# One more weight unit loaded during the output product, norm rows prepared on GpSimd among the experts, and eighteen units in single transfers

## The chip, the cores and the metric

The kernel runs on one core of a Trainium2 chip. A core has a matrix engine (TensorE, PE in the profile; its weight loads are listed as PEld), a vector engine (VectorE, DVE), a scalar engine (ScalarE, ACT), a general engine (GpSimd, POOL) and a sync engine (SyncE, SP) that here only issues transfers. Sixteen DMA engines move data between the large memory (HBM) and the on-chip memory (SBUF). Each engine runs its own list of instructions in order, and semaphores hold an instruction back until what it needs is there. Matrix products are accumulated in a small memory of banks (PSUM), from which DVE or ACT copy ("evict") them.

The metric is the device time of one execution in microseconds (us); lower is better.

## The reference

One encoder layer on 512 tokens of width 1024, in float32. Three token mixers run side by side (neighbourhood attention, grouped-query attention with rotary positions, attention to 256 memory tokens). Their outputs are gated, summed and multiplied by `w_out`; a residual and a layer norm follow. Then comes the mixture of experts, another residual and another layer norm:

```
merged = sum_g sigmoid(gate_g(x)) * (branch_g @ w_branch[g])
x = layer_norm(DN_ALPHA * x + merged @ w_out, ln1_g, ln1_b)

aff = softmax(x @ w_router)                  # 512 x 16
gate, idx = top_k(aff.T, 64)                 # every expert picks its 64 tokens
xs = x[idx]                                  # 16 x 64 x 1024
h  = xs @ w_gate_up                          # 16 experts, 1024 x 2048 each
y  = (silu(h[:, :1024]) * h[:, 1024:]) @ w_down   # 1024 x 1024 each
x  = layer_norm(DN_ALPHA * x + scatter_add(gate * y), ln2_g, ln2_b)
```

The weights of the sixteen experts are 192 MB in float32, read once each. The four vectors `ln1_g`, `ln1_b`, `ln2_g`, `ln2_b` (the "norm rows") are needed at the ends of both residuals; the host hands them over as 15 rows of 1024, named `lnp`.

## The kernel before

**Stages.** The mixers fill the first part of the execution, up to about 450 us. The output product (`woc`, L1108 to L1112) and, in between its pieces, the router (logits, the top 64 of each expert, one-hot matrices) follow until about 517 us. The expert stage then runs from expert 0 to expert 15, and a final layer norm ends at 962.1 us. All instructions are written out by hand in the order in which each engine runs them; no planner moves them.

**Weight units.** The expert weights are cut into 192 units of 1 MB, each 128 partitions x 2048 numbers: per expert eight units "gu" (a slice of gate and up) and four "dn" (a slice of down). `_blocks()` (L45) lists them in the order of use, where the down product of expert e-1 stands in the middle of the gate/up product of expert e: gu0 0-7, gu1 0-3, dn0 0-3, gu1 4-7, gu2 0-3, dn1 0-3, gu2 4-7, gu3 0-3, dn2 0-3, gu3 4-7, gu4 0-3 and so on. Counted from 0, gu2 2 is unit 22.

**The ring.** The units go into slots which are buffers that the mixers used and no longer need. `RING` (L32) names them: twelve places with room for one or two units, 22 units in all. The first round is loaded during the mixers and the output product, as each place comes free. Three places later leave (`ROUNDS`: "raw" after one round, "VS" and "G1" after two), so 18 slots remain. `Ring.load` (the transfer is L829) issues the next load on SP; `Ring.done` (L850) is called where a unit has been used, and issues the next load as soon as its slot is free. Most loads bring two units in one transfer of 2 MB (a pair), which needs both slots of a place; early units (below 36) and the last ten come in single transfers of 1 MB. Loads wait in SP's list in ring order, each for the PE instructions that last read its slot, and for the landing of the transfer that stands eight before it.

**The pause.** Around the output product SP issues a load into "raw" at 475.70 us, and the next one, into "Q9", at 501.80 us, when the output product has released that buffer.

**The experts.** For expert e, `gate_up` (PE lines L1314: tiles g and u) multiplies the 64 gathered tokens with the gu units. `act_h` (L1319) makes the hidden values: ACT a tanh (L1324, tile tg), DVE two products (L1325 into tg, L1326 into h). `h_transpose` turns h and `down` (PE L1350, tile y) multiplies with the dn units. Before every fourth expert, `gather` (PE L1274 and L1276, tile ga) collects the tokens of the next four experts by one-hot products in eight chunks; they go through three PSUM buffers ("mm"), and their evictions into xs are shared between DVE (L1281) and ACT (L1279). gather(1), for experts 4 to 7, stands right after `act_h(3)` in the program. The tiles tg and h come from the tag "t", which has two buffers that are taken in turn.

**The norm rows.** `load_norms` loads the 15x1024 rows during the mixers into a buffer there; one ACT copy (`norm_hi`, L877) and two DVE operations (`norm_mask` L881, `norm_lo` L884) split them into a high and a low part in the tile gb. Their first use is `ln_row` (PE L1398) in expert four, from 617.3 us.

**Router scratch.** The tile rt (tag "bf") holds the router's small tables. Later "bf" holds GTe, the transposed one-hot matrices of an expert pair made by `slots_T`.

Of the kernel before, what the change touches and what calls it, by code (L numbers as in the profile page):

```python
# [9 lines left out]
F32 = mybir.dt.float32  # L10
# [8 lines left out]
P = 128  # L19
# [25 lines left out]
def _blocks():  # L45
    order = []
    for e in range(NEXP - 1):
        order += [("gu", e, k) for k in range(lead(e))]
        if e:
            order += [("dn", e - 1, k) for k in range(4)]  # L50
        order += [("gu", e, k) for k in range(lead(e), KD)]
    order += [("gu", NEXP - 1, k) for k in range(KD)]
    order += [("dn", e, k) for e in (NEXP - 2, NEXP - 1) for k in range(4)]
    blocks, i, r = [], 0, 0
    while i < len(order):
        for tag, n in RING:
            left = ROUNDS.get(tag, len(order)) - r
            if left > 0 and i < len(order):
                keys = order[i:i + n]
                i += n  # L60
                if r and (i < FULL or i > len(order) - N_SINGLE):
                    blocks += [(tag, h, [key]) for h, key in enumerate(keys)]
                else:
                    blocks.append((tag, 0, keys))
        r += 1
    return blocks

# [2 lines left out]
def layer_kernel(ctx: ExitStack, tc: tile.TileContext, xt, xn, first0, wu, bgate, rpb, gains, wrt,  # L70
# [194 lines left out]
    gb = cp.tile([15, D], F32R, name="gb")  # L265
# [186 lines left out]
    def g_gqa():  # L452
        kk = R("Q6", [P, 4, S], "kk", F32R)
        qs = R("Q4", [P, 8, S], "qs", F32R)
        ST["b01"] = b01 = R("Q5", [P, 4, 1024], "ropevg")
        b1t = b01[:, 2:4]
        vg = b1t[:, 0, :512].rearrange("p (m f) -> p m f", m=NT)
        ST.update(khh=kk[:, 0:2], klo=kk[:, 2:4], vg=vg, qs=(qs[:, 0:4], qs[:, 4:8]),
                  rope=(vs_t[:, 0], b1t[:, 1]), zr=b01[:, 0:2])
        rope = []  # L460
        for q in range(3):
            us = ws.take(2)
            zs = ST["A5" if q % 2 else "A6"][:, 1, :512 if q == 0 else 1024].rearrange("p (m c) -> p m c", m=NT)
# [12 lines left out]
        a, b = rope[1:]  # L476
        bg.extend([lambda: None, a[4], b[0], a[5], b[1], b[2], b[3], norm_hi, b[4], b[5]])

    def g_na_v():
        v = ST["b01"][:, 0:2].rearrange("p a (b f) -> p (a b) f", f=S)  # L480
# [333 lines left out]
    class Ring:  # L814
# [7 lines left out]
        def load(self):  # L822
            tag, h, keys = self.blocks[self.n]
            n = len(keys)
            src = wx[self.row:self.row + P * n].rearrange("(p j) (h c) -> p (j h) c", j=n, h=2)
            if tag not in self.home:
                self.home[tag] = R(tag, [P, 2 * dict(RING)[tag], D], f"w{self.n}")
            full = self.home[tag][:, 2 * h:2 * (h + n)]
            nc.sync.dma_start(full, src)  # L829
# [35 lines left out]
        after[N_UNITS - 14 + 2 * i] = [lambda: ring.more(4)]  # L865
    vs_t = R("VS", [P, 2, 1024], "ropesq")

    norm_raw = []

    def load_norms():  # L870
        norm_raw.append(vs_t[:15, 1])
        nc.sync.dma_start(norm_raw[0], lnp)

    after[14] = [load_norms]

    def norm_hi():
        nc.scalar.copy(gb, norm_raw[0])  # L877

    def norm_mask():
        norm_raw.append(vs_t[:15, 0])  # L880
        nc.vector.tensor_scalar(norm_raw[1], gb.bitcast(F32), gb_c, None, op0=ALU.mult)  # L881

    def norm_lo():
        nc.vector.scalar_tensor_tensor(gb, norm_raw[0], gb_s, norm_raw[1], op0=ALU.mult, op1=ALU.add)  # L884


    run(g_mem())
    dump("mkT", ST["mkT"])
# [9 lines left out]
    bg.extend([norm_mask, norm_lo])  # L898
    run(g_branch(2, True), 1.0, 3)
    run(g_na_v(), 1.0)  # L900
    at.drain()
# [15 lines left out]

    run(g_branch(1, False, between), 0.5)

    rt = R("bf", [P, 12, 64], "rt")  # L920
    aff = rt[:, 0].rearrange("p (m e) -> p m e", m=NT)
    cnt = rt[:, 2:4].rearrange("p a (m e) -> p m a e", m=NT)
    st_all = rt[:, 5:7].rearrange("p a b -> p (a b)")[:, :96].rearrange("p (m q s) -> p m q s", m=NT, q=4)
    ones_f = rt[:, 7:9].rearrange("p a b -> p (a b)")
    nc.gpsimd.memset(ones_f, 1.0)
    lgA = rt[:, 9].rearrange("p (m e) -> p m e", m=NT)
    rb = rt[:, 10][:, :NEXP]
    wsum = rt[:, 10][:, NEXP:3 * NEXP].rearrange("p (a e) -> p a e", a=2)
# [3 lines left out]
    wg_t = rt[:, 2:4].rearrange("p a (k e) -> p (a k) e", e=NEXP)  # L932
    wb_t = rt[:, 0:2].rearrange("p a (k e) -> p (a k) e", e=NEXP)
    wps = []

    def router_scale():
        for i, w in enumerate((wg_t, wb_t)):
# [14 lines left out]
    at.drain()  # L952
    dump("ynh", ST["y0"][0].bitcast(F32))
    dump("macc", ST["macc"])


    mh = R("G0", [P, KD, S], "mh", F32R)
# [24 lines left out]
    tri_t = [rt[:, 4].bitcast(F16), rt[:, 11].bitcast(F16), tri_d]  # L982
# [13 lines left out]
    a01 = R("t", [48, P], "a01", bufs=2)  # L996
    a23 = R("t", [48, 64 + P], "a23", bufs=2)
    nc.gpsimd.memset(a01, 0.0)
    nc.gpsimd.memset(a23, 0.0)
    top = cp.tile([48, 64], F32, name="top")  # L1000

    eps2 = small([P, 2], "eps", bufs=1)
# [5 lines left out]
    mvs, rs_v, rs_h, rs_y, rs_a, nmx, sme, rce = (  # L1008
        small([P, NT, 2] if n == "mv" else [P, NT], "r_" + n, bufs=1) for n in ("mv", "v", "h", "y", "a", "nm", "sm", "rc"))

    def r_transpose(m, k0, n=4):
        t = R("tmp", [P, n, P], f"x1T{m}{k0}", bufs=2)
        tp = PB("T", f"x1t{m}{k0}", (P, n, P))
        for j in range(n):
            k = k0 + j
# [110 lines left out]
    us = ws.take(2)  # L1126
    ws.prefetch(2)
    us += ws.take(2)
    ring.upto(8)

    def w_rest(m, c, n, q, hooks={}):
        acc = PB("S", f"woc{m}{c}")
# [72 lines left out]
    x1_norm(3)  # L1205
    x1_parts(3)
    keep_warm(28)
    ring.upto(len(RING))
    dump("aff", aff)


# [93 lines left out]
    def gate_up(e, ks):  # L1305
# [3 lines left out]
        for k in ks:  # L1309
            w = ring.get("gu", e, k)  # L1310
            xs = XS[qd][k // 4][:, k % 4, i * CAP:(i + 1) * CAP]
            for b in range(2):
                for hf in range(2):
                    nc.tensor.matmul(GU[e][b][hf * 64:hf * 64 + 64], xs,  # L1314
                                     w[b][:, hf * 512:hf * 512 + 512],
                                     start=(k == 0), stop=(k == KD - 1))
            ring.done("gu", e, k)

# [9 lines left out]
    def h_transpose(e, tp=None):  # L1328
# [2 lines left out]
        for c in range(4):  # L1331
            nc.tensor.transpose(tp[:, c], h[:, c * P:(c + 1) * P], ident)  # L1332
        if e == 0:
            homes.extend((R("tmp", [P, 4, P], "hT", bufs=2), R("tmp", [P, NT, P], "GT", F32R, bufs=2)))
# [42 lines left out]
    def slots_T(pr):  # L1377
        qd, h = divmod(pr, 2)
        gp = PB("mm", f"gT{pr}", (P, NT, P))
        for m in range(NT):  # L1380
            nc.tensor.matmul(gp[:, m], OH[qd][:, m, h * P:(h + 1) * P], id16, start=True, stop=True)
        if pr == 0:
            homes.append(R("bf", [P, NT, P], "GTe", F32R))
        g = homes[1 if pr % 2 else 2]
        GT[pr] = g
        nc.scalar.copy(g, gp)

# [2 lines left out]
    def acc_of(m):  # L1390
# [2 lines left out]
            ACC.update({0: a[:, 0:2], 1: a[:, 2:4]})  # L1393
        return ACC[m // 2][:, m % 2]

    def ln_row(row, h, nm):
        bc = PB("mm", nm)
        nc.tensor.matmul(bc, gsel[:, row:row + 1].to_broadcast([15, P]), gb[:, h * 512:h * 512 + 512], start=True, stop=True)  # L1398
        return bc

    def residual():
# [57 lines left out]
    def last_down(g2, xq):  # L1459
# [81 lines left out]
            nc.vector.tensor_tensor(c[:, :, 2], nm[:, p], c[:, :, 0].bitcast(F32), op=ALU.subtract)  # L1541

        def low_rank(m, h):
            nc.tensor.matmul(tl[m, h], rows[m // 2][:13, m % 2], gb[:13, h * 512:h * 512 + 512], start=bool(h), stop=True)

        rows = {}

# [80 lines left out]
    onehot(0, 2, 2)  # L1628
    g1 = gather(0, 2, 2)
    side = iter(())  # L1630
    for e in range(NEXP):
        if e == 0:
            for k in range(KD):
# [3 lines left out]
        elif e < NEXP - 1:  # L1637
# [216 lines left out]
```

## Time and profile before

| what | value |
|---|---|
| time, median of 3 runs | 964.44 us (964.22 to 966.48) |
| the profiled execution | 963.93 us, of which the span is 962.1 us |
| mean granted clock of PE | 0.998 |
| PE busy | 944.4 us, 98% of the span |
| DVE, ACT, POOL busy | 454.0, 278.1, 88.5 us |
| weight loads on SP (L829) | 83 of 2 MB, 26 of 1 MB |
| all transfers | 251.17 MB, 261 GB/s over the span |

Busy times are summed over the whole span, and the stages differ much: the mixers keep PE, DVE and ACT at work with few transfers, the expert stage is products and weight transfers. The rows below come from the page and from answers of the trace. A row of a timeline is start, duration, engine, line, operation, tiles (out<-in), shapes and count; in brackets stands the idle time of the engine just before it and what ended it. `SPq` rows are the issues of transfers by SP. A row of waits is who waited for what: total us, times, longest. A row of windows is the stretch, its length, then the busy time (and count) of PE, PEld, DVE, ACT and POOL, the granted clock, the share of the DMA engines and GB/s.

### The profile page before, as it was taken

What the parts mean: (1) busy time and instruction counts of PE and PEld (TensorE: products, weight loads), DVE (VectorE), ACT (ScalarE), POOL (GpSimd) and SP (SyncE); (2) the same over time, 40 slices, a digit from 0 to 9 for tenths busy, and PEclk for the clock granted to TensorE, in tenths of its full rate; (3) what the DMA queues carried; (4) which work ended last, traced back from release to release, by engine and by line L of the source; (5) the groups of instructions that cost most, each with busy time, mean ns of one, the idle gap of its engine ahead of it and who ended that gap; (6) DMA issues with size and microseconds to landing.
All of it is one profiled execution on the core that took longest, in us unless ns stands there. A gap on an engine that the chain in (4) does not pass through costs nothing.

```text
span 962.1 us, 12945 instructions
## 1 busy us (share of the span) xinstructions
PE 944.4 (98%) x5270; PEld 609.2 (63%) x5270; DVE 454.0 (47%) x857; ACT 278.1 (29%) x546; POOL 88.5 (9%) x103
## 2 busy tenths in 40 slices
PE   9999999999999999999999999999999999998997
PEld 9899878888888888887885333433344333432345
DVE  6347668874376566237454121643322223231426
ACT  6334454543344454333242111100010000100123
POOL 0102303000032231000023000000000000000004
PEclk9999999999999999999999999999999999999999
DMA  9321211211433322565919999999999999999992
GB/s 361 116 67 67 66 66 44 66 52 60 115 93 103 100 83 77 217 275 204 386 35 389 428 419 429 432 428 433 428 430 431 430 429 432 429 432 430 428 421 109
DMA packets 39192, 251.17 MB, mean 261 GB/s; under 512 B 13007, under 2 KB 13391, under 8 KB 24926
## 3 DMA queue, kind: packets, MB, share of 16 engines
q1 hardware_dynamic: 38702, 250.26, 64.7%
q8 instruction: 41, 0.67, 0.3%
q10 hardware_dynamic: 432, 0.10, 0.0%
q14 instruction: 17, 0.14, 0.0%
HBM read 247.46 MB, written 2.10 MB: 259 GB/s over the span
## 4 chain that ended last, share of the span: by engine, by line
PE 84%; DMA 8%; DVE 4%; POOL 1%; ACT 1%; issue 1%; DVEq 0%; POOLq 0%; ACTq 0%; SPq 0%
PE g L1314 10%; PE u L1314 9%; PE y L1350 9%; DMA w<-in_wx 8%; PE gate L282 4%; PE gate L283 4%; PE gate L284 4%; PE pr L282 2%; PE pr L283 2%; PE pr L284 2%; PE gy L670 2%; PE ga L1274 2%; PE nqk L282 2%; PE nqk L283 2%; PE nqk L284 2%; PE gt L657 1%
## 5 line engine op out<-in xcount | busy, mean ns | idle before, releaser
L1314 PE MATMUL g<-w,xs 128*64 128x512 f32 x512 | 135.0, 606 | 2.5 <-DMA w<-in_wx 2.4
L1314 PE MATMUL u<-w,xs 128*64 128x512 f32 x512 | 131.6, 592 | 0.0
L1350 PE MATMUL y<-w,hT 128*64 128x512 f32 x480 | 106.6, 594 | 3.1 <-DMA w<-in_wx 2.4
L1314 PEld LDWEIGHTS u<-w,xs 128*64 128x64 f32 x512 | 36.8, 137 | 73.1 <-issue 72.3
L98 DVE TENSOR_TENSOR los<-raw_twin,whi 128x1024 fp32r<-128x1024 f32 x42 | 53.6, 1277 | 59.4 <-ACT whi L97 59.2
L98 DVE TENSOR_TENSOR y<-y,y 64x512 fp32r<-64x512 f32 x28 | 19.3, 689 | 129.8 <-ACT y L97 120.4
L97 ACT CAST y<-y 64x512 fp32r<-64x512 f32 x28 | 16.2, 579 | 217.3 <-PE y L1350 206.8
L1350 PEld LDWEIGHTS y<-w,hT 128*64 128x64 f32 x480 | 33.9, 137 | 71.3 <-issue 65.0
L284 PE MATMUL gate<-xh,los 128*128 128x512 f32 x192 | 74.8, 390 | 0.0
L1314 PEld LDWEIGHTS g<-w,xs 128*64 128x64 f32 x512 | 30.7, 136 | 53.5 <-issue 45.0
L282 PE MATMUL gate<-xh,whi 128*128 128x512 f32 x144 | 57.2, 397 | 0.0
L283 PE MATMUL gate<-xl,whi 128*128 128x512 f32 x144 | 56.1, 390 | 0.0
L1433 DVE TENSOR_TENSOR acc<-acc,cb 128x512 f32<-128x512 f32 x56 | 35.6, 683 | 37.8 <-PE cb L1431 37.8
L1513 POOL TENSOR_TENSOR acc<-acc,ln2g 128x512 f32<-128x512 f32 x8 | 10.0, 1275 | 427.8 <-ACT y L97 427.3
L97 ACT CAST whi<-raw_twin 128x1024 fp32r<-128x1024 f32 x42 | 44.1, 1049 | 9.4 <-PE wo L1112 4.3
L284 PEld LDWEIGHTS gate<-xh,los 128*128 128x128 f32 x192 | 36.0, 188 | 7.7
L98 DVE TENSOR_TENSOR los<-raw_twin,los 128x1024 fp32r<-128x1024 f32 x20 | 25.0, 1248 | 26.3 <-ACT los L97 26.2
L646 ACT ACTIVATE att_twin<-gs,nm 128x512 f32<-128x512 f32 x32 | 21.7, 683 | 49.0 <-DVE nm L645 49.0
L1324 ACT ACTIVATE tg<-g 128x512 f32<-128x512 f32 x16 | 9.5, 596 | 88.9 <-PE g L1314 88.9
L1337 DVE COPY hT<-ht 128x512 f32<-128x512 f32 x15 | 10.4, 690 | 44.4 <-PE ht L1332 44.4
L282 PEld LDWEIGHTS gate<-xh,whi 128*128 128x128 f32 x144 | 27.0, 188 | 6.6 <-issue 1.2
L283 PEld LDWEIGHTS gate<-xl,whi 128*128 128x128 f32 x144 | 27.1, 188 | 5.3
(448 smaller groups left out, 1876.5 us busy)
## 6 DMA issues: line engine op xcount, KB each, us to landing
w<-in_wx SPq DMA_DIRECT2D x83, 2048.0 KB
raw_twin<-in_wu SPq DMA_DIRECT2D x65, 512.0 KB
w<-in_wx SPq DMA_DIRECT2D x26, 1024.0 KB
raw<-in_wu SPq DMA_DIRECT2D x8, 512.0 KB
xr<-in_xt SPq DMA_DIRECT2D x4, 512.0 KB
macc<-in_xn SPq DMA_DIRECT2D x2, 1024.0 KB
out<-acc SPq DMA_DIRECT2D x8, 256.0 KB
first<-in_first SPq DMA_DIRECT2D x4, 384.0 KB
```

Source lines behind the costliest of these rows:

```text
L97: nc.scalar.copy(hi, src)
L98: nc.vector.tensor_tensor(lo, src, hi.bitcast(F32), op=ALU.subtract)
L282: nc.tensor.matmul(acc, w_h, rh[:, k], start=(k == 0), stop=False)
L283: nc.tensor.matmul(acc, w_h, rl[:, k], start=False, stop=False)
L284: nc.tensor.matmul(acc, w_l, rh[:, k], start=False, stop=(k == nk - 1))
L646: nc.scalar.activation(self.p[:, h], self.s[h], AF.Exp, bias=nm[:, h:h + 1], accum_out=self.sm[:, h:h + 1])
L670: nc.tensor.matmul(self.y[h * 64:h * 64 + 64, :P], ST["vg"][:, kc, kvh * 64:kvh * 64 + 64], self.pt[:, h, kc], start=(kc == 0), stop=(kc = ...
L1274: nc.tensor.matmul(g, XH[:, m, c], oh[:, m, sl], start=(m == 0), stop=False)
L1314: nc.tensor.matmul(GU[e][b][hf * 64:hf * 64 + 64], xs, w[b][:, hf * 512:hf * 512 + 512], start=(k == 0), stop=(k == KD - 1))
L1337: nc.vector.tensor_copy(t, tp)
L1350: nc.tensor.matmul(y[o * 64:o * 64 + 64], hT[:, c, hf * 64:hf * 64 + 64], w[j][:, o * 512:(o + 1) * 512], start=(k == 0 and j == 0), stop= ...
L1433: nc.vector.tensor_tensor(a, a, cb, op=ALU.add)
```

## The change

1. **Unit X.** A block "X" is put behind "raw" in the first round. It holds one unit, the one after the 22 of the ring (unit 22, gu2 2), in three buffers outside the ring: wxc (128x1024, new tag "gb", whose place gb occupied), wxa (128x512, tag "bf") and wxb (128x512, tag "tmp"). It is loaded by three transfers on SP between the "raw" and the "Q9" load. Its place isn't filled again. All later units move by one place in the ring.
2. **Singles.** Blocks whose units end at index 50 to 67 (the places Q5, Q7, Q4, Q3, Q6, Q9, M, Q2 and Q1) are loaded as 18 transfers of 1 MB instead of nine of 2 MB.
3. **Norm rows.** The load and its three operations leave the mixers. `norm_rows()` does them in two halves of 15x512, the first around the middle of expert two, the second in expert three: a transfer on SP (emitted before the last gate/up unit ahead of the down product; in SP's list the first stands behind the load into M, the second behind the two singles into Q3), and after the down product four GpSimd operations (copy, two scalar products, a sum). The raw rows and the scratch are taken from "t", so they stand in turn with tg and h: nraw0 follows tg1, npart0 follows h1, and tg2 and h2 follow these; nraw1 follows tg2, npart1 h2, and tg3 and h3 follow these.
4. **Buffers of the router.** Since wxa holds "bf", the router's tables move to "t", `lnT` and a small tile; x1T alternates between "tmp" and "oh"; the one-hot transposes of pair 0 move from expert one to expert two.

```diff
-                if r and (i < FULL or i > len(order) - N_SINGLE):
+                if r and (i < FULL or 50 <= i < 68 or i > len(order) - N_SINGLE):
...
+        if r == 0:
+            blocks.insert([t for t, _, _ in blocks].index("raw") + 1, ("X", 0, order[i:i + 1]))
+            i += 1
...
+            if tag == "X":
+                key, = keys
+                g = [R("bf", [P, 512], "wxa"), R("tmp", [P, 512], "wxb", bufs=2)]
+                u = R("gb", [P, D], "wxc")
+                nc.sync.dma_start(u, src[:, 1])
+                nc.sync.dma_start(g[1], src[:, 0, 512:])
+                nc.sync.dma_start(g[0], src[:, 0, :512])
+                self.t[key] = [g, u]
...
-    after[14] = [load_norms]
-
-    def norm_hi():
-        nc.scalar.copy(gb, norm_raw[0])
-
-    def norm_mask():
-        norm_raw.append(vs_t[:15, 0])
-        nc.vector.tensor_scalar(norm_raw[1], gb.bitcast(F32), gb_c, None, op0=ALU.mult)
-
-    def norm_lo():
-        nc.vector.scalar_tensor_tensor(gb, norm_raw[0], gb_s, norm_raw[1], op0=ALU.mult, op1=ALU.add)
...
-    rt = R("bf", [P, 12, 64], "rt")
+    wtmp = R("bf", [P, 6, 64], "wtmp")
...
+    rt, rt1 = (R("t", [P, 8, 64], n, bufs=2) for n in ("rt", "rt1"))
...
-    ring.upto(8)
+    ring.upto(9)
...
-        if pr == 0:
-            homes.append(R("bf", [P, NT, P], "GTe", F32R))
-        g = homes[1 if pr % 2 else 2]
+        if pr < 2:
+            homes.append(R("tmp", [P, NT, P], "GT", F32R, bufs=2) if pr else R("bf", [P, NT, P], "GTe", F32R))
+        g = homes[1 + pr % 2]
...
+    def norm_rows():
+        GB.append(R("gb", [15, D], "gb", F32R))
+        for h in range(2):
+            c = slice(h * 512, h * 512 + 512)
+            raw = R("t", [15, 512], f"nraw{h}", bufs=2)
+            nc.sync.dma_start(raw, lnp[:, c])
+            yield
+            part = R("t", [15, 512], f"npart{h}", bufs=2)
+            nc.gpsimd.tensor_copy(GB[0][:, c], raw)
+            nc.gpsimd.tensor_scalar(part, GB[0][:, c].bitcast(F32), gb_c, None, op0=ALU.mult)
+            nc.gpsimd.tensor_scalar(raw, raw, gb_s, None, op0=ALU.mult)
+            nc.gpsimd.tensor_tensor(GB[0][:, c], raw, part, op=ALU.add)
+            yield
...
                 if k == lead(e) - 1:
                     h_transpose(e - 1)
+                    if e in (2, 3):
+                        steps(nrm)
                 gate_up(e, (k,))
...
-            if e % 2:
-                slots_T(e // 2)
+            if e % 2 and e > 1 or e == 2:
+                slots_T((e - 1) // 2)
...
             for k in range(lead(e), KD):
+                if e in (2, 3) and k == lead(e):
+                    steps(nrm)
                 gate_up(e, (k,))
```

More of the change, by code (lines that the diff above doesn't have):

```diff
@@ L264, in layer_kernel @@
     nc.sync.dma_start(lnT[:, :2], lnt)
-    gb = cp.tile([15, D], F32R, name="gb")
     gb_s, gb_c, gb_t = (cp.tile([15, n], F32, name="gb_" + k)[:, :1] for k, n in (("s", 1), ("c", 1), ("t", 33)))
@@ L476, in g_gqa @@
         a, b = rope[1:]
-        bg.extend([lambda: None, a[4], b[0], a[5], b[1], b[2], b[3], norm_hi, b[4], b[5]])
+        bg.extend([lambda: None, a[4], b[0], a[5], b[1], b[2], b[3], lambda: None, b[4], b[5]])
     def g_na_v():
@@ L825, in load @@
             src = wx[self.row:self.row + P * n].rearrange("(p j) (h c) -> p (j h) c", j=n, h=2)
+            if tag == "X":
[6 more added lines that the diff above has]
+                self.t[key] = [g, u]
+                self.at[key] = (tag, 0)
+                self.row += P
+                self.n += 1
+                return
             if tag not in self.home:
@@ L866, in layer_kernel @@
     vs_t = R("VS", [P, 2, 1024], "ropesq")
[L868 to L872, printed above, removed]
-    after[14] = [load_norms]
-    def norm_hi():
-        nc.scalar.copy(gb, norm_raw[0])
-    def norm_mask():
-        norm_raw.append(vs_t[:15, 0])
-        nc.vector.tensor_scalar(norm_raw[1], gb.bitcast(F32), gb_c, None, op0=ALU.mult)
-    def norm_lo():
-        nc.vector.scalar_tensor_tensor(gb, norm_raw[0], gb_s, norm_raw[1], op0=ALU.mult, op1=ALU.add)
     run(g_mem())
@@ L897, in layer_kernel @@
     at.add([GqaUnit(hp, m) for hp in range(4) for m in range(NT)])
-    bg.extend([norm_mask, norm_lo])
+    bg.extend([lambda: None, lambda: None])
     run(g_branch(2, True), 1.0, 3)
@@ L918, in layer_kernel @@
     run(g_branch(1, False, between), 0.5)
-    rt = R("bf", [P, 12, 64], "rt")
[L921 to L924, printed above, removed]
+    wtmp = R("bf", [P, 6, 64], "wtmp")
+    wb_t = wtmp[:, 0:2].rearrange("p a (k e) -> p (a k) e", e=NEXP)
+    ones_f = wtmp[:, 2:4].rearrange("p a b -> p (a b)")
     nc.gpsimd.memset(ones_f, 1.0)
-    lgA = rt[:, 9].rearrange("p (m e) -> p m e", m=NT)
-    rb = rt[:, 10][:, :NEXP]
-    wsum = rt[:, 10][:, NEXP:3 * NEXP].rearrange("p (a e) -> p a e", a=2)
+    wsum = wtmp[:, 4][:, :2 * NEXP].rearrange("p (a e) -> p a e", a=2)
+    rb = lnT[:, 2:4].rearrange("p a k -> p (a k)")
+    wg_t = wr_t
     tri_d = cp.tile([P, P], F16, name="tri_d")
@@ L931, in layer_kernel @@
     nc.gpsimd.memset(ones_h, 1.0)
-    wg_t = rt[:, 2:4].rearrange("p a (k e) -> p (a k) e", e=NEXP)
-    wb_t = rt[:, 0:2].rearrange("p a (k e) -> p (a k) e", e=NEXP)
     wps = []
     def router_scale():
-        for i, w in enumerate((wg_t, wb_t)):
+        for i, w in ((1, wb_t), (0, wg_t)):
             nc.vector.tensor_tensor(w, wr_t, lnT[:, i, :, None].to_broadcast([P, KD, NEXP]), op=ALU.mult)
@@ L954, in layer_kernel @@
     dump("macc", ST["macc"])
+    rt, rt1 = (R("t", [P, 8, 64], n, bufs=2) for n in ("rt", "rt1"))
+    aff = cp.tile([P, NT, NEXP], F32, name="aff")
+    cnt = rt[:, 0:2].rearrange("p a (m e) -> p m a e", m=NT)
+    st_all = rt[:, 4:6].rearrange("p a b -> p (a b)")[:, :96].rearrange("p (m q s) -> p m q s", m=NT, q=4)
+    ones_f = rt[:, 6]
+    nc.gpsimd.memset(ones_f, 1.0)
+    lgA = rt1[:, 0].rearrange("p (m e) -> p m e", m=NT)
+    a01 = rt1[:48, 2:4].rearrange("p a b -> p (a b)")
+    a23 = rt1[:48, 4:7].rearrange("p a b -> p (a b)")
+    nc.gpsimd.memset(a01, 0.0)
+    nc.gpsimd.memset(a23, 0.0)
     mh = R("G0", [P, KD, S], "mh", F32R)
@@ L980, in lo_part @@
         nc.vector.scalar_tensor_tensor(ml[:, j], tmp, 0.5, mh[:, j].bitcast(F32), op0=ALU.mult, op1=ALU.subtract)
-    tri_t = [rt[:, 4].bitcast(F16), rt[:, 11].bitcast(F16), tri_d]
+    tri_t = [rt[:, 2].bitcast(F16), rt[:, 3].bitcast(F16), tri_d]
     for i in range(3):
@@ L995, in layer_kernel @@
     run(g_na_proj())
[L996 to L999, printed above, removed]
     top = cp.tile([48, 64], F32, name="top")
@@ L1009, in layer_kernel @@
         small([P, NT, 2] if n == "mv" else [P, NT], "r_" + n, bufs=1) for n in ("mv", "v", "h", "y", "a", "nm", "sm", "rc"))
+    x1T = [R("tmp", [P, 4, P], "x1T", bufs=2), R("oh", [P, 4, P], "x1To")]
     def r_transpose(m, k0, n=4):
-        t = R("tmp", [P, n, P], f"x1T{m}{k0}", bufs=2)
+        x1T.append(x1T.pop(0))
+        t = x1T[0][:, :n]
         tp = PB("T", f"x1t{m}{k0}", (P, n, P))
@@ L1207, in layer_kernel @@
     keep_warm(28)
-    ring.upto(len(RING))
+    ring.upto(len(RING) + 1)
     dump("aff", aff)
@@ L1314, in gate_up @@
                     nc.tensor.matmul(GU[e][b][hf * 64:hf * 64 + 64], xs,
-                                     w[b][:, hf * 512:hf * 512 + 512],
+                                     w[b][hf] if isinstance(w[b], list) else w[b][:, hf * 512:hf * 512 + 512],
                                      start=(k == 0), stop=(k == KD - 1))
@@ L1333, in h_transpose @@
         if e == 0:
-            homes.extend((R("tmp", [P, 4, P], "hT", bufs=2), R("tmp", [P, NT, P], "GT", F32R, bufs=2)))
+            homes.append(R("tmp", [P, 4, P], "hT", bufs=2))
         t = R("bf", [P, 4, P], f"hT{e}") if e == NEXP - 1 else homes[0]
@@ L1394, in acc_of @@
         return ACC[m // 2][:, m % 2]
+    GB = []
+    def norm_rows():
[11 more added lines that the diff above has]
+            yield
     def ln_row(row, h, nm):
         bc = PB("mm", nm)
-        nc.tensor.matmul(bc, gsel[:, row:row + 1].to_broadcast([15, P]), gb[:, h * 512:h * 512 + 512], start=True, stop=True)
+        nc.tensor.matmul(bc, gsel[:, row:row + 1].to_broadcast([15, P]), GB[0][:, h * 512:h * 512 + 512], start=True, stop=True)
         return bc
@@ L1543, in low_rank @@
         def low_rank(m, h):
-            nc.tensor.matmul(tl[m, h], rows[m // 2][:13, m % 2], gb[:13, h * 512:h * 512 + 512], start=bool(h), stop=True)
+            nc.tensor.matmul(tl[m, h], rows[m // 2][:13, m % 2], GB[0][:13, h * 512:h * 512 + 512], start=bool(h), stop=True)
         rows = {}
@@ L1630, in layer_kernel @@
     side = iter(())
+    nrm = norm_rows()
     for e in range(NEXP):
```

## The prediction

> **Bounds.** I read the page first (busy time, slices, chain), then the stages by windows, then the chain's last links and the waits.
>
> ```profile
> span 962.1 us, 12945 instructions
> PE 944.4 (98%) x5270; PEld 609.2 (63%) x5270; DVE 454.0 (47%) x857; ACT 278.1 (29%) x546; POOL 88.5 (9%) x103
> PE   9999999999999999999999999999999999998997
> PE 84%; DMA 8%; DVE 4%; POOL 1%; ACT 1%; issue 1%; DVEq 0%; POOLq 0%; ACTq 0%; SPq 0%
> ```
> PE (TensorE) is busy for 944.4 of 962.1 us, and the slices show no hole until the last three. By that alone only less PE work would help. The windows say more; their columns are length, busy time of PE, PEld, DVE, ACT and POOL, granted clock, DMA share and GB/s.
>
> ```profile
> 483.00:501.00 18.00, 18.00 (x122) 16.30 (x121) 10.62 (x45) 5.77 (x14) 3.65 (x14) 1.00 0.01 2
> 519.00:530.00 11.00, 11.00 (x78) 4.38 (x76) 1.01 (x3) 0.91 (x2) 0.00 (x0) 1.00 0.98 375
> 530.00:580.00 50.00, 50.00 (x288) 18.25 (x286) 10.47 (x27) 6.78 (x14) 0.00 (x0) 1.00 1.01 424
> 607.00:880.00 273.00, 271.73 (x1347) 107.99 (x1344) 92.87 (x160) 28.52 (x50) 0.00 (x0) 1.00 1.01 431
> 880.00:922.00 42.00, 37.70 (x166) 13.12 (x168) 12.92 (x20) 5.55 (x10) 0.00 (x0) 1.00 1.01 429
> ```
> In the expert stage the DMA engines are as full as PE: share 1.01, 431 GB/s, so a weight unit of 1 MB (1.049e6 bytes) takes 2.43 us. Before it, from 483 to 501 us, they move 2 GB/s: 18 us are unused. In the last window PE is 37.7 busy of 42. There the weights run late:
>
> ```profile
> PE g L1314 <- DMA w<-in_wx: 2.4, 4, 1.2
> PE y L1350 <- DMA w<-in_wx: 2.4, 2, 1.2
> ```
> ```profile
> 841.83 33.64 DMA w<-in_wx
> 875.54 38.76 DMA w<-in_wx
> ```
> The first fence is the waits from 840 to 946 us (total, times, longest), the second the chain's only two long DMA links. PE loses 4.8 us to late weights, and what ends last from 841.83 to 914.3 is a stream of transfers. So the end is set by when the stream began, its bytes, and every hole in it. PE's own work could end at most 4.8 us sooner.
>
> **Part 1.** Unit X goes into the pause (a gain).
>
> ```profile
> 475.70 0.33 SPq L829 DMA_DIRECT2D w<-in_wx  x1
> 501.80 0.33 SPq L829 DMA_DIRECT2D w<-in_wx  x1
> SPq L829 <- PE woc L1111: 25.7, 1, 25.7
> ```
> SP issued the "raw" load at 475.70 and then stood 25.7 us behind the output product (woc) to 501.80. X's three transfers are issued between the two, for 3 x 0.33 us of an SP that waits anyway. Their buffers come free in the router's preparation, ahead of 475.70, so X lands in the empty 18 us. It needs no slot of the ring: the load that a given finished unit releases now brings the unit after the one that it used to bring. The stream keeps its times and carries one unit fewer: -2.43 us. Bounds: -2.0 if pairs that straddle other unit boundaries wait a little longer, -2.7 if a little of the 375 GB/s refill at 519 to 530 us is regained. The end may not gain more than PE's 4.8 us allows, which doesn't bind.
>
> **Part 2.** Units 50 to 67 come as 18 single loads instead of 9 pairs. Each is released by its own unit, up to one unit sooner. It costs 9 more issues of 0.33 us on SP, hidden while SP mostly waits for PE. The stream is at 424 to 431 GB/s around them already, so I take 0; bounds -0.4 (half of the 50 us at 424 brought to 431) and +0.3 (one more issue late).
>
> **Part 3.** From the attention stage one 60 KB load, one ACT, two DVE operations go; PE has no hole there for them to have caused (the row of nines): 0. The router's scratch tiles change buffers, GTe's transposes (eight PE rows) move from expert one to two: same work, and PE is 50.00 of 50 busy there, 0 +-0.2.
>
> **Part 4.** The norm rows move to experts two and three (a cost). The half rows are loaded by SP behind weight loads, worked on by four GpSimd operations of 15x512 each, and use the rotating "t" buffers. The second half, nraw1, sits in the buffer that tg3 takes next. So expert three's tanh (L1324) now waits for the last GpSimd operation, which waits for the transfer. When does that land? Nraw1 is issued right behind the load that stood at 588.15.
>
> ```profile
> 566.82 0.33 SPq L829 DMA_DIRECT2D w<-in_wx  x1
> 588.15 0.33 SPq L829 DMA_DIRECT2D w<-in_wx  x1
> 845.26 0.33 SPq L829 DMA_DIRECT2D w<-in_wx  x1
> ```
> ```profile
> 880.36 1.08 PE L1314 MATMUL g<-w,xs 128*64 128x512 f32 x4 [0.60 <-DMA w<-in_wx]
> ```
> The load issued at 845.26 is noticed by the PE wait that ends at 880.36. It is 56 loads of 2 MB (117.4e6 bytes) after the one of 588.15: at the windows' 429 to 431 GB/s 272.5 to 273.7 us, taken as 273.2. So the load of 588.15 is complete at about 607.2. A small transfer does not overtake:
>
> ```profile
> 16.74 0.39 SPq L252 DMA_DIRECT2D consts<-in_gains  x1
> 25.34 1.41 POOL L253 TENSOR_SCALAR consts<-consts 128x64 f32<-128x64 f32 x1 [24.06 <-DMA consts<-in_gains]
> 26.74 0.26 POOL L258 TENSOR_SCALAR consts<-consts 128x24 f32<-128x24 f32 x1
> L1097 POOL CAST xhl<-macc 128x1024 f16<-128x1024 f32 x2 | 2.1, 1036 | 2.8 <-ACT macc L1094 2.8
> L1100 POOL TENSOR_TENSOR xhl<-macc,xhl 128x512 f16<-128x512 f32 x8 | 9.0, 1155 | 0.2
> L535 POOL TENSOR_TENSOR macc<-macc,tm 128x512 f32<-128x512 f32 x8 | 13.9, 1742 | 77.2 <-DVE tm L534 77.2
> ```
> 64 KB issued at 16.74 behind other loads reached GpSimd at 25.34. So nraw1 arrives at about 607.2. Then copy 0.52 (half of L1097), two scalar operations between 0.26 (L258) and 1.41 (L253), taken as 0.6 since one input is what the copy has too, and a sum of 1.16 (L1100): about 3.0 us, bounds 2.2 and 5.6 (1.04 + 2 x 1.41 + 1.74). It runs to 610.2.
>
> The Trainium skill, "GPSIMD Engine Reference", section "3.1 Elementwise — side-by-side cycle accounting", puts 512 one-input elements at 769 ns and two-input ones at 2.6 cycles each, an estimate of 3 x 0.77 + 1.1 = 3.4 us for the four; by it the sum below would be 0.4 us higher.
>
> ```profile
> 605.69 0.60 ACT L1324 ACTIVATE tg<-g 128x512 f32<-128x512 f32 x1 [3.97 <-PE g L1314]
> 607.78 0.54 DVE L1281 TENSOR_SCALAR xs<-ga,gT,lnT 128x256 f32<-128x256 f32 x1
> 609.06 0.60 PE L1274 MATMUL ga<-oh,xhl 128*128 128x256 f16 x4
> 613.70 0.65 PE L1314 MATMUL g<-w,xs 128*64 128x512 f32 x2
> 592.33 0.33 SPq L829 DMA_DIRECT2D w<-in_wx  x1
> 604.82 0.33 SPq L829 DMA_DIRECT2D w<-in_wx  x1
> 615.68 0.33 SPq L829 DMA_DIRECT2D w<-in_wx  x1
> ```
> Tanh stood at 605.69, so it is 4.5 us late. Behind it on ACT and DVE, in order, stand tg's two products and the evictions of gather(1). PE's fourth gather chunk (609.06) needs a buffer that the first eviction (607.78 + 0.54 = 608.32) frees: 0.74 to spare. PE then stands 4.5 - 0.7 = 3.8 us (2.8 to 6.2).
>
> Does that reach the end? Expert four's first unit (613.70) is consumed 3.8 us later, and so is the slot of the load near 615.68. Between it and the load of 588.15 stand three (the first at 592.33, the last at 604.82: 6 MB, 14.6 us), noticed by 621.8, which is 6.1 us after 615.68. A start from empty costs something:
>
> ```profile
> 502.00:508.50 6.50, 5.36 (x45) 4.68 (x44) 4.51 (x21) 5.29 (x11) 5.53 (x7) 1.00 0.88 329
> ```
> From the issue at 501.80, 2.14 MB had moved by 508.5: 6.7 us, where the full stream takes 5.0. With 1.7 for that, the spare time lies between 0 and 4.4 us; no row shows a smaller lead that kept the stream whole, and the wait for the notice is in it, so I take 1.1. The stream then has a hole of 3.8 - 1.1 = 2.7 us (0 to 6.2), never made up, since it is full to the end.
>
> The first half is covered. It follows the load of 566.82, six loads (29.2 us) ahead: landed 578.0, done 581.0.
>
> ```profile
> 583.87 0.60 ACT L1324 ACTIVATE tg<-g 128x512 f32<-128x512 f32 x1 [4.10 <-PE g L1314]
> ```
> Tanh of expert two stood at 583.87: 2.9 us to spare, enough even with 5.6 us of GpSimd but for 0.3.
>
> **Sum.** -2.43 + 0 + 0 + 2.7 = +0.3 us. The profiled execution took 963.93 (span 962.1, 1.8 around it), 0.5 below the median of 964.44: 964.2 against it, 964.7 against the median.
>
> **The rivals.**
> The wait is covered: faster. If nraw1 overtakes the backlog, or the four operations are short and the ring's spare time is near its 4.4 us, the hole vanishes and the gain of X stays: 964.44 - 2.43 = 962.0, with Part 2's -0.4 or X's -2.7 at best 961.3. For it: 18 singles make finer steps, and the spare time is uncertain by 4.4 us. Against it: the 8.6 us of the gains' transfer. It wins where the PE stall is under the spare time.
>
> The clock drops in the stall: slower.
>
> ```profile
> 956.48 0.39 PE L1544 MATMUL lr<-gb,rows 13*128 13x512 f32 x1
> 956.00:958.00 2.00, 0.87 (x4) 0.36 (x2) 1.41 (x2) 1.26 (x2) 0.00 (x0) 1.00 0.77 300
> 958.00:960.00 2.00, 0.00 (x0) 0.00 (x0) 0.00 (x0) 0.00 (x0) 0.00 (x0) 0.74 1.04 400
> 960.00:962.00 2.00, 0.00 (x0) 0.00 (x0) 0.00 (x0) 0.00 (x0) 0.00 (x0) 0.50 0.23 86
> ```
> PE's last product ends at 956.87; the clock is 1.00 to 958 and 0.50 from about 958.96 (0.74 as a mean), so 2.1 us of idling on top of a thin stretch sufficed. A 3.8 us hole at 609 could do the same. Half speed for as long as the hole lasted costs 1.9 us more, all of it hole in the stream: 966.6, and 967.8 with the GpSimd sum 1.2 us dearer. Against it: PE is full right before 609, and no row shows a hole that long between full work. It decides once the stall outlasts the clock's patience. The Trainium skill, "TensorE: Matmul & The Clock Gate", section "What's actually happening", has the clock halved after an idle window of about 3.4 us, free running; by that a 3.8 us stall is at the edge. The trace's 2.1 us after thin work neither refutes nor proves it.
>
> X does not land in the pause: no gain. If its issue stays behind a busy buffer till 501.80, it only joins the stream: 964.44 + 2.7 = 967.1. Against it: nothing of the router's preparation is still at work on those buffers at 475.70.
>
> **How the numbers follow.** Hole as reckoned 0.48 (964.7; its own range 963.2 to 966.9); covered 0.22 (962.0); clock 0.18 (966.6 to 967.8); X late 0.06 (967.1); anything else 0.06, both ways. A measurement tells about 0.3% from no change here: below 961.55 is faster, above 967.33 slower. The covered case reaches faster only with its extras: 0.13 with a share of the rest. Slower takes half of the clock case, half of X late, dear GpSimd work and a share of the rest: 0.2. The remainder, 0.67, is same. The range 961.7 to 967.6 leaves about 0.1 on each side.
>
> **What the profile after would show.** X right: three transfers issued between 476 and 478 us, DMA traffic in the pause, and the waits for weights from 840 us on moved by one unit. The cost right: POOL busy between 607 and 610, "ACT tg <- POOL" at expert three, a PE hole of about 3.8 us in gather(1), and a dip in GB/s near 620 us. Expert two's tanh without a wait for POOL. PEclk below 1.00 near 610 would mean the clock case. I am wrong if the hole is there and the GB/s do not dip (more spare time), or if the hole is much longer or absent.

## The result, and the profile after

The changed kernel takes 968.59 us (median of 10 runs, 966.12 to 971.63); the kernel before took 964.58 in the same comparison (10 runs, 964.15 to 966.48). The ratio is 1.0038, 95% interval 1.0029 to 1.0047: by the medians the change makes it 4.0 us slower, where 964.7 was forecast and the range ended at 967.6. The profiled execution has a span of 967.0 us instead of 962.1.

From the page of the changed kernel, its busy times and the transfer rate in 40 slices:

```profile
span 967.0 us, 12994 instructions
PE 945.7 (98%) x5270; PEld 610.0 (63%) x5270; DVE 451.7 (47%) x855; ACT 277.4 (29%) x545; POOL 97.4 (10%) x112
GB/s 359 113 66 66 66 66 49 61 67 44 115 122 77 97 82 87 241 270 182 400 94 383 428 413 425 351 410 432 431 430 430 431 430 431 430 431 430 429 419 101
```

X's three transfers are issued right behind the load into "raw" (476.07), and the stretch from 483 to 501 us, which moved 2 GB/s before, now moves 40 (the first part of X has landed by 483):

```profile
476.44 0.43 SPq L832 DMA_DIRECT2D wxc<-in_wx  x1
476.91 0.44 SPq L833 DMA_DIRECT2D wxb<-in_wx  x1
477.45 0.40 SPq L834 DMA_DIRECT2D wxa<-in_wx  x1
```
```profile
483.00:501.00 18.00, 18.00 (x121) 16.27 (x119) 10.30 (x44) 5.42 (x14) 3.68 (x14) 1.00 0.10 40
```

Slices 26 and 27 of the page (counted from 1) hold 351 and 410 GB/s where the neighbours have 425 to 432: that is the hole in the stream of weights, between 604 and 653 us. What makes it, from the timeline of the changed kernel between 604 and 622 us (GpSimd, ACT, PE and SP):

```profile
607.45 0.60 POOL L1408 CAST gb<-nraw 15x512 fp32r<-15x512 f32 x1 [24.54 <-DMA nraw<-in_lnp]
608.15 1.55 POOL L1409 TENSOR_SCALAR npart<-gb,gb_c 15x512 f32<-15x512 f32 x1
609.70 1.55 POOL L1410 TENSOR_SCALAR nraw<-nraw,gb_s 15x512 f32<-15x512 f32 x1
611.33 1.25 POOL L1411 TENSOR_TENSOR gb<-nraw,npart 15x512 fp32r<-15x512 f32 x1
...
612.62 0.60 ACT L1326 ACTIVATE tg<-g 128x512 f32<-128x512 f32 x1 [10.57 <-POOL gb L1411]
613.11 0.56 ACT L1281 ACTIVATE xs<-ga,lnT,gT 128x256 f32<-128x256 f32 x1
...
613.72 1.01 PE L1276 MATMUL ga<-oh,xhl 128*128 128x256 f16 x4 [4.17 <-ACT xs L1281]
620.03 1.08 PE L1316 MATMUL g<-w,xs 128*64 128x512 f32 x4
...
606.87 0.33 SPq L843 DMA_DIRECT2D w<-in_wx  x1
622.00 0.33 SPq L843 DMA_DIRECT2D w<-in_wx  x1
```

Read it downward. The second half of the norm rows reaches GpSimd at 607.45. GpSimd works on it until 612.58. The tanh of expert three (605.69 before) starts at 612.62, and behind it on ACT comes the eviction of gather(1)'s second chunk. PE waits 4.17 us for that. The first unit of expert four follows at 620.03 instead of 613.70, and the load which its slot was to take is issued at 622.00. SP issued nothing from 606.87 to then.

The windows of the changed kernel show that PE also ran slow after the hole, and how empty the DMA engines got. The last row is the same stretch of the kernel before.

```profile
610.00:613.00 3.00, 0.00 (x0) 0.00 (x0) 0.00 (x0) 0.38 (x1) 2.50 (x2) 1.00 1.03 434
613.90:617.10 3.20, 3.20 (x17) 2.21 (x16) 1.69 (x4) 0.56 (x1) 0.00 (x0) 0.50 1.01 428
617.50:620.00 2.50, 2.50 (x31) 2.26 (x28) 0.92 (x2) 0.61 (x2) 0.00 (x0) 1.00 0.95 403
620.00:624.00 4.00, 4.00 (x22) 1.35 (x19) 3.70 (x11) 0.52 (x1) 0.00 (x0) 1.00 0.32 98
620.00:621.00 1.00, 1.00 (x10) 0.41 (x9) 0.80 (x6) 0.52 (x1) 0.00 (x0) 1.00 0.35 147
621.00:622.00 1.00, 1.00 (x8) 0.37 (x6) 0.94 (x5) 0.00 (x0) 0.00 (x0) 1.00 0.02 8
622.00:623.00 1.00, 1.00 (x6) 0.29 (x4) 1.00 (x2) 0.00 (x0) 0.00 (x0) 1.00 0.19 33
623.00:624.00 1.00, 1.00 (x6) 0.29 (x2) 0.96 (x1) 0.00 (x0) 0.00 (x0) 1.00 0.70 205
626.00:627.00 1.00, 1.00 (x8) 0.62 (x8) 1.00 (x2) 0.00 (x0) 0.00 (x0) 1.00 0.55 148
607.00:632.00 25.00, 20.07 (x122) 10.75 (x121) 14.61 (x24) 2.75 (x5) 4.95 (x4) 0.93 0.86 349
```
```profile
607.00:632.00 25.00, 24.25 (x148) 11.74 (x146) 14.71 (x25) 3.29 (x6) 0.00 (x0) 1.00 1.01 432
```

For 3.2 us the granted clock is 0.50: PE's work of 1.6 us took 3.2. The stream moves 349 instead of 432 GB/s for 25 us, which is 83 x 25 / 432 = 4.8 us of transfer lost; the stretch from 632 to 700 us loses 0.8 us more (425 against 430). The rows of single microseconds show that the restart costs no less than the empty stretch: the loads run out between 620 and 621, the next is issued at 622.00, the stream moves 33 and 205 GB/s in the two microseconds behind that, and 148 once more at 626. With 2.4 us gained by X, 4.8 + 0.8 - 2.4 = 3.2 us are accounted for, of 4.0 between the medians and of 4.9 between the two profiled spans. The rest is not assigned; profiled executions already stand up to 2.0 us apart before the output product (the load into "raw" was issued at 475.70 before, at 476.07 here, between 475.01 and 477.03 in the versions below).

### The profile page after: what moved, and what is told of

It reads as the page before. It is cut to its first block, busy times and chain, and to the rows that moved or that the text cites. A ratio compares the mean times of both kernels' runs of the same rounds, so it can differ in the third digit from the quotient of the medians.

```text
span 967.0 us, 12994 instructions
## 1 busy us (share of the span) xinstructions
PE 945.7 (98%) x5270; PEld 610.0 (63%) x5270; DVE 451.7 (47%) x855; ACT 277.4 (29%) x545; POOL 97.4 (10%) x112
```

## The experiments

The theory to test (A) had three parts by then: the wait of the tanh for GpSimd makes the hole in PE, the hole drops the clock, and the stream loses nearly all of both; X itself brings its 2.4 us. The rival (B) put the loss on the eighteen single loads or the moved buffers.

**Norm rows wholly in expert two** (`early`). Both halves are loaded into the two "t" buffers in expert two, where GpSimd's work is done by ACT and DVE; expert three has none of it.

```diff
-            raw = R("t", [15, 512], f"nraw{h}", bufs=2)
-            nc.sync.dma_start(raw, lnp[:, c])
-            yield
-            ...
+        raw = [R("t", [15, 512], f"nraw{h}", bufs=2) for h in range(2)]
+        for h in range(2):
+            nc.sync.dma_start(raw[h], lnp[:, h * 512:h * 512 + 512])
+        yield
+        g = [GB[0][:, h * 512:h * 512 + 512] for h in range(2)]
+        for h in range(2):
+            nc.scalar.copy(g[h], raw[h])
+        for h in range(2):
+            nc.vector.tensor_scalar(g[h], g[h].bitcast(F32), gb_c, None, op0=ALU.mult)
+            nc.vector.scalar_tensor_tensor(g[h], raw[h], gb_s, g[h].bitcast(F32), op0=ALU.mult, op1=ALU.add)
```

> The change with both norm halves loaded and prepared in expert two, by ACT (two copies) and DVE (two scalar products, two sums), so that nothing of them is left in expert three; X and the single loads stay. Theory A (the tanh of expert three waiting for GpSimd, and the clock drop in the hole that it makes, are the whole loss): no PE hole in gather(1), clock 1.00 and about 430 GB/s from 607 to 625 us, time 964.6 - 2.4 for X + 0.4 to 0.8 that the stream was already late before the stall = 962.6 to 963.0. Rival B (the single loads or the moved buffers make the hole in the stream): a dip near 620 us remains, time 966 or more.

Measured: 962.42 us (12 runs), ratio to the kernel before 0.9979 (0.9970 to 0.9988). Its window from 607 to 632 us:

```profile
607.00:632.00 25.00, 24.24 (x150) 11.88 (x148) 14.71 (x24) 3.32 (x6) 0.00 (x0) 1.00 1.02 429
```

PE is as full as before the change, the clock is 1.00 and the stream nearly whole (429 against 432 GB/s). X, the singles and the buffers stayed and did no harm, so rival B is out. The version moves the transfer and also changes the engines; `late_dve` below tells the two apart. It is about 2 us faster than the kernel before.

**Without X** (`nox`: the block "X" is not inserted, all else as changed).

> The change without unit X: ring and order of units as before, norm rows on GpSimd and single loads as changed. If X brings its 1 MB out of the stream: 968.6 + 2.4 = 971.0. If X brought nothing: 968.6.

Measured: 969.9 us (6 runs, ratio 1.0057, 1.0045 to 1.0069), only 1.3 us above the changed kernel. By itself that doesn't show the worth of X, since the removal also moves the small transfer: in its profiled execution the second half reached GpSimd at 610.49, 3.0 us later than in the changed kernel, and PE's hole was 6.91 us. The stream moved 333 instead of 349 GB/s from 607 to 632 us, 0.9 us more lost. X's 2.4 and these 0.9 us fit the profiled spans (970.5 against 967.0), but not the medians: the forecast of 971.0 was missed, and why the other executions are nearer isn't known. The clean form is the next one.

**Without X and without the wait** (`early_nox`: the same removal in `early`).

> The version with the norm rows wholly in expert two, without unit X. Theory A: X is worth its 2.4 us of stream and the rest nothing: 962.4 + 2.4 = 964.8, level with the kernel before (964.6). If the moved router buffers or the norm work cost something by themselves, it stands above 964.6 by that: 965.2 or more.

Measured: 964.7 us (11 runs), ratio 1.0000 (0.9992 to 1.0009). X is worth 964.7 - 962.42 = 2.3 us (the intervals of the two ratios don't overlap), and router buffers, single loads and the norm rows in this form together cost nothing that shows.

**Same place, faster engines** (`late_dve`).

```diff
-            nc.gpsimd.tensor_copy(GB[0][:, c], raw)
-            nc.gpsimd.tensor_scalar(part, GB[0][:, c].bitcast(F32), gb_c, None, op0=ALU.mult)
-            nc.gpsimd.tensor_scalar(raw, raw, gb_s, None, op0=ALU.mult)
-            nc.gpsimd.tensor_tensor(GB[0][:, c], raw, part, op=ALU.add)
+            nc.scalar.copy(GB[0][:, c], raw)
+            nc.vector.tensor_scalar(part, GB[0][:, c].bitcast(F32), gb_c, None, op0=ALU.mult)
+            nc.vector.scalar_tensor_tensor(GB[0][:, c], raw, gb_s, part, op0=ALU.mult, op1=ALU.add)
```

> The change with the same transfers and places of the norm halves, but ACT (copy, about 0.6 us) and DVE (product and sum, about 0.7 us each) in place of the four GpSimd operations, which took 5.13 us in the changed kernel. The transfer still lands at about 607.4 us. Theory A (the wait's length sets the loss, one to one): tanh of expert three at about 609.5 instead of 612.6, PE hole in gather(1) about 1 to 1.5 us instead of 4.17, no clock drop there, time 962.4 + 1.0 to 1.6 = 963.4 to 964.0. Rival (the late transfer is the cost, whatever works on it): 967 or more.

Measured: 963.72 us (12 runs), ratio 1.0002 (0.9988 to 1.0015). ACT and DVE need 0.62, 0.47 and 0.74 us where GpSimd needed 0.60, 1.55, 1.55 and 1.25:

```profile
606.77 0.62 ACT L1408 CAST gb<-nraw 15x512 fp32r<-15x512 f32 x1 [4.93 <-DMA nraw<-in_lnp]
608.78 0.60 ACT L1326 ACTIVATE tg<-g 128x512 f32<-128x512 f32 x1 [1.40 <-DVE gb L1410]
609.88 0.60 PE L1276 MATMUL ga<-oh,xhl 128*128 128x256 f16 x4 [0.55 <-ACT xs L1281]
611.46 0.60 PE L1276 MATMUL ga<-oh,xhl 128*128 128x256 f16 x4 [0.54 <-DVE xs L1283]
```

Two holes of 0.55 us are left of the 4.17. The transfer comes nearly as late as in the changed kernel (606.77 against 607.45), so its lateness alone is cheap: with the shorter work behind it, it costs 1.3 us against `early`; the five microseconds of GpSimd behind it are not. The times reach from 962.73 to 968.48, and the three above 967 have a mean clock of 0.995 or 0.996 where the others have 0.998 or 0.999. What happened in these three isn't known: none of them was profiled.

**Longer wait** (`pool3`: the first scalar product of the second half four times).

> The change with the first scalar product of the second half done four times instead of once: 3 x 1.55 = 4.65 us more on GpSimd ahead of the tanh of expert three. Theory A: the PE hole grows by the same 4.65 us and the end by about as much, 968.6 + 4.65 = 973.2 (972 to 974.5, since the clock may stay low longer). Rival (the stream had spare time left or the hole is hidden): under 971.

Measured: 972.15 us (4 runs), ratio 1.0089 (1.0072 to 1.0105): 3.6 us for 4.65 us of GpSimd. The forecast of 972 to 974.5 holds, at its low end. PE's hole grew from 4.17 to 8.86 us, one to one:

```profile
617.38 1.01 PE L1276 MATMUL ga<-oh,xhl 128*128 128x256 f16 x4 [8.86 <-ACT xs L1281]
```

**Filled hole** (`warm`: 17 identity products on PE between the third and fourth chunk of gather(1)).

```diff
+            if qd == 1 and f == 2:
+                idle = PB("Y", "idle")
+                for _ in range(17):
+                    nc.tensor.matmul(idle[:, :P], ident, ident, start=True, stop=True)
```

> The change with 17 identity products put on PE between the third and the fourth chunk of gather(1), into the unused Y bank: about 4 us of work where PE stood idle for 4.17 us. Theory A (the hole itself drops the clock, 0.50 from about 613.9 to 617.1 us, and that costs 1.6 us more): clock 1.00 throughout, fourth chunk at the same time, first unit of expert four 1.6 us sooner, time 968.6 - 1.6 = 967.0, and less scatter between runs. Rival (the low clock is hidden by the evictions, which are then the limit): time stays at 968.6.

Measured: 968.55 us (7 runs, 965.72 to 972.58), ratio 1.0042 (1.0025 to 1.0060): by the median the rival's number, so the 1.6 us are not shown by the times. The profiled execution does as A says:

```profile
608.90 3.96 PE L1287 MATMUL idle<-ident 128*128 128x128 f32 x34
614.36 0.60 PE L1276 MATMUL ga<-oh,xhl 128*128 128x256 f16 x4 [0.55 <-DVE xs L1283]
618.12 1.08 PE L1320 MATMUL g<-w,xs 128*64 128x512 f32 x4
```

The clock stays at 1.00, four products (half a chunk) take 0.60 instead of 1.06 us, and expert four starts at 618.12 instead of 620.03. The stream moves 368 instead of 349 GB/s from 607 to 632 us, which is 1.1 us; that execution took 965.72. The four runs with a mean clock of 0.999 or 0.998 took 965.7 to 968.6, the three at 0.995 to 0.997 took 968.8 to 972.6. Where the clock dropped in those three isn't known. Counted by the span from first to last instruction, the median of the seven is 965.9, against 966.8 for the changed kernel; the execution of 968.55 has a span of 965.9 and 2.65 us around it, where most have 1.8. So the price of the low clock lies somewhere between nothing and 1.6 us; these runs don't fix it.

**Pairs instead of singles** (`nosingles` on the changed kernel, `early_nosingles` on `early`: the condition `50 <= i < 68` removed).

> The change with units 50 to 67 in pairs again. Theory A (single loads are neutral but for where the stream has run dry): the load behind the hole needs two freed slots again and comes up to one unit (1.7 to 2.4 us) later, time 968.6 to 970.5. Rival B (eighteen single transfers, each waiting for the landing of the one eight before it, hold the stream back): 966 to 967.5 and a smaller dip near 620 us.

> The version with the norm rows wholly in expert two, with units 50 to 67 in pairs again. Where no hole is left, theory A has the single loads neutral: 962.4, within 0.5. If singles by themselves cost (more issues, eight-transfer wait) or gain (finer steps), it moves by 0.5 or more to one side.

Measured: 969.77 us (6 runs, ratio 1.0057, 1.0043 to 1.0071) against 968.59; and 963.49 us (11 runs, ratio 0.9987, 0.9979 to 0.9996) against 962.42. In both, pairs are 1.1 us dearer, and the intervals just overlap. The profile of `early_nosingles` has a place for it:

```profile
607.00:632.00 25.00, 24.24 (x149) 11.70 (x146) 14.81 (x25) 3.19 (x6) 0.00 (x0) 1.00 0.99 405
```

405 GB/s instead of 429 (`early`) for 25 us are 1.4 us of the stream, with PE equally full. Rival B is out: nothing became faster with pairs. The singles seem to help a little, where theory A had them neutral in `early`. They belong to X, which shifts the units by one: expert four starts at about the same time (613.80, before the change 613.70), but the pair that was issued at 615.68, behind its first unit, now waits for its second and is issued at 617.49.

**The scatter** (`early_fill`, `early_fill2`). In the profile of `early`, PE's old hole near 120 us, where the transposes of the first rotary query pair wait for GpSimd, was followed by a low clock. The timeline row of `early` shows the hole, and two windows the clock: first `early`, then the kernel before, which has the same hole (1.79 us). Eleven of the twelve profiled executions have this hole, of 1.79 to 1.84 us; the clock fell in this one only.

```profile
121.72 1.00 PE L426 MATMUL rT<-ident,ropevg 128*128 128x128 f32 x4 [1.84 <-POOL ropevg L420]
```
```profile
119.00:128.00 9.00, 7.16 (x27) 5.57 (x26) 4.15 (x6) 1.20 (x3) 2.66 (x2) 0.81 0.17 58
```
```profile
119.00:128.00 9.00, 7.21 (x35) 5.72 (x34) 4.68 (x6) 2.63 (x7) 2.98 (x2) 1.00 0.17 58
```

Both versions put eight identity products (1.95 us) on PE, the second one in the right place, in `heads_T`:

```diff
+            if q == 1 and pair == 0:
+                for _ in range(8):
+                    nc.tensor.matmul(tp[:, 0], ident, ident, start=True, stop=True)
```

> The version with the norm rows wholly in expert two, with eight identity products on PE ahead of the first transposes of the rotary keys, where PE stands idle for 1.8 us near 120 us. In the profiled run of the version without them the clock was 0.50 from about 121.9 to 125.4 us after that hole, and the run stood 1.3 us behind by 449 us; in the kernel before the same hole left the clock at 1.00. If a hole of 1.8 us can drop the clock in some executions: no execution with a mean clock of 0.996 or less, slowest time under 964.5 (966.05 without the products), median 962.0 to 962.4. If the scatter comes from elsewhere: single executions at 965 to 966 remain.

Measured: 962.63 us (11 runs, 962.02 to 963.11), ratio 0.9981 (0.9972 to 0.9990). The condition there was `q == 0`, and the products went ahead of transposes near 91 us: the hole of 1.79 us at 120 us stayed, so this version says nothing on the hole, though its times scatter by 1.1 us only.

> The same eight identity products, now ahead of the transposes of the first rotary query pair, where the hole of 1.8 us near 120 us stands (ahead of the rotary keys, near 91 us, they left that hole as it was: 1.79 us). The products take 1.95 us, so the hole is filled and nothing is held up by more than 0.2 us. If the hole of 1.8 us drops the clock in some executions: clock 1.00 from 119 to 128 us, every execution at a mean clock of 0.998 or more, none above 964.5, median 962.0 to 962.6. If the scatter comes from elsewhere: single executions at 965 to 966 with a mean clock of 0.996 remain.

Measured: 961.3 us (5 runs, 960.69 to 962.17), ratio 0.9962 (0.9948 to 0.9975), every run with a mean clock of 0.998 or 0.999. PE is 8.94 of 9 us busy there:

```profile
119.00:128.00 9.00, 8.94 (x51) 7.61 (x50) 4.73 (x6) 2.57 (x6) 3.39 (x2) 1.00 0.18 59
```

It is the fastest version here. That the filled hole is the reason fits, but isn't proved: `early_fill` has the hole open and the mean clock at 0.998 or 0.999 in all its runs too, and five runs are few.

## Why the prediction was wrong

The step that failed is the last one of part 4, the hole in the stream of weights: 2.7 us were put into the sum, 3.8 us of standing PE less 1.1 us to spare. The runs showed 5.6 us (4.8 from 607 to 632 us, 0.8 behind). PE came to expert four 6.3 us late, not 3.8, since the clock fell in the hole, which the sum put at nothing, and nearly all of that reached the stream.

What bounds the kernel: right as far as the runs go. `pool3` loses more of the stream (266 GB/s from 607 to 632 us) and ends later, `early` keeps nearly all of it (429) and ends earlier.

Part 1, X: right. -2.43 us was forecast, 2.3 us measured (`early_nox` against `early`).

Part 2, the singles at 0 (+0.3 to -0.4): probably wrong by a little. The medians give them 1.1 us in both pairs of runs, with intervals that just overlap; without them X's shift of the units makes a pair wait for one unit more.

Part 3, moved work at 0: right (`early_nox` 1.0000, with the norm rows in their early form).

Part 4, the mechanism: right in its links, wrong in one reading and in sizes.

- The landing was forecast for 607.2, GpSimd started at 607.45. The small transfer, issued at 590.63 behind weight loads, did arrive with them.
- The first half is covered, as forecast, but with less to spare: GpSimd was done at 582.92 instead of 581.0, and the tanh of expert two at 584.26 still waited for PE alone.
- GpSimd: 3.0 us forecast, 5.13 measured. The dear part is the scalar product: 0.6 us taken "since one input is what the copy has too", 1.55 measured. The row L253 (1.41 us for an operation of that kind, on 64 numbers a row) came nearest, and stood in the prediction as the dear bound. The Trainium skill's best case of 769 ns for 512 elements ("GPSIMD Engine Reference", section "3.1 Elementwise — side-by-side cycle accounting") is half of what this scalar product takes; its 2.6 cycles an element for two inputs (an estimate of 1.1 us) agree better with the measured 1.25.
- The hole in PE: 3.8 us forecast, 4.17 measured, by luck: two errors nearly cancel. The dearer GpSimd work adds 2.1 us. But the fourth chunk needs the buffer of the second chunk, which ACT evicts right behind the tanh (from 613.11 to 613.67), and not that of the first, which DVE evicts two operations later (from 614.71). That takes about 1.6 us off.
- The spare time: 1.1 us taken from 0 to 4.4, with 0 called the end that the rows support. PE came 6.3 us late to expert four, and the stream lost 5.6: net, the spare time was about 0.7 us. The stream did run on until about 620 us, 4.5 us past the 615.68 of the kernel before, but the restart cost 3.6 us or so (the hole of 5.6 less the empty stretch of about 2), not the 1.7 that the prediction read from the start at 501.80. It isn't a fixed number of the kernel either: in `nox`, where the units aren't shifted, PE came 9.8 us late (623.53 against 613.70) and the stream lost 6.5 (333 instead of 432 GB/s from 607 to 632 us, 412 instead of 430 to 650 us).
- The clock: given 0.18 as a rival, at 966.6 to 967.8. It was the case. Every run of the changed kernel has a mean clock of 0.995 to 0.997 (0.998 before in the profiled execution), and 613.90 to 617.10 shows 0.50. PE lost 1.6 us by it in the profile, where 1.9 was forecast; what it costs at the end `warm` leaves open. The row that the prediction read for it (clock down 2.1 us after the last product) was a weak guide: at the ends of the twelve profiled executions the clock falls between 0.4 and 3.3 us after the last product. In the holes of the changed kernel and of `pool3` and `nox` it fell 4.2, 3.3 and 4.5 us after PE had stopped. By the Trainium skill, "TensorE: Matmul & The Clock Gate", section "What's actually happening", an idle window of about 3.4 us halves the clock; the hole of 4.17 us agrees, and the drop after 1.84 us in one run of `early` is shorter than that figure.

So the sum should have read: -2.4 for X and 5.6 for the hole in the stream, about +3.2, where +0.3 stood and 4.0 was measured. The 5.6 follow from PE's 6.3 us (4.2 of hole, 1.6 of clock, the rest mostly a later start of the gather) less 0.7 to spare. The last 0.8 us stay open.

## What to carry to other kernels

Where transfers and TensorE are both full, a wait has little cover: cost it at its full length unless a row shows spare time, add the restart of the transfers, and price a clock drop into the sum when TensorE would stand for about 4 us (here it cost PE 1.6 us). A small load issued behind a backlog of large ones arrived with the backlog here, so load it a stage earlier, and put what works on it on the engine that is fastest for it, before a buffer that the critical chain rotates through is needed again. When two durations of an operation differ five times in the profile, price the new one by the dearer until its kind is known.

## What the runs showed that was not expected

A hole of 1.84 us in TensorE's work was followed by a granted clock of one half for about 3.5 us in one execution (0.81 as the mean from 119 to 128 us), and the same hole left it at 1.00 in ten others. So the length of a hole alone doesn't say whether the clock falls. It doesn't explain the scatter of the times either: they spread over 5.5 us for the changed kernel and 6.9 us for `warm`, but over 1.1 us for `early_fill`, which has this hole too. On GpSimd a scalar product with one scalar per row took 1.55 us for 15x512, two and a half times the copy of the same size (0.60) and more than the sum of two tensors (1.25); DVE took 0.47 us for it.
